# A two-layer encoder on one core: the last quarter of a norm's shift and scale read after the norm, and three up groups interleaved token-major

## The chip, the core and the metric

The kernel runs on one NeuronCore of a Trainium2 chip. A core has TensorE (PE, matrix products, with its weight loads shown apart as PEld), VectorE (DVE), ScalarE (ACT), GpSimd (POOL) and SyncE (SP), which here issues nearly all DMA transfers. Each engine runs its own instructions in a fixed order and waits for others by semaphores. The metric is the device time of one execution in microseconds (us); the number for a kernel is the median of its runs.

## The reference

The model has two layers over 256 tokens of width D = 2048, all in float32. A conditioning vector c sets, for each layer, six vectors of length 2048: shift, scale and gate for the mixer (m) and for the feed-forward part (f).

```python
c_act = jax.nn.silu(c)
for l in range(DEPTH):
    mod = (c_act @ w_mod[l] + b_mod[l]).reshape(bn, 6, d)
    shift_m, scale_m, gate_m = mod[:, 0, None], mod[:, 1, None], mod[:, 2, None]
    shift_f, scale_f, gate_f = mod[:, 3, None], mod[:, 4, None], mod[:, 5, None]
    h = layer_norm(x) * (1.0 + scale_m) + shift_m
    proj = h @ w_in[l]
    ...
    y = jnp.concatenate([y_a, y_b, y_c, y_d], axis=-1) @ w_out[l]
    x = layer_norm(ALPHA * x + (1.0 + gate_m) * y, post_mix_g[l], post_mix_b[l])
    h = layer_norm(x) * (1.0 + scale_f) + shift_f
    y = conv_ffn(h, w_up[l], w_conv[l], b_conv[l], w_down[l])
    x = layer_norm(ALPHA * x + (1.0 + gate_f) * y, post_ffn_g[l], post_ffn_b[l])
```

`conv_ffn` multiplies h by w_up (2048 by 11264), splits the result into a gate and a value half of 5632 columns, runs a causal convolution of width 3 and a SiLU over the gate half, multiplies the two halves and multiplies by w_down. w_mod has 2048 rows and 12288 columns a layer, 100 MB in float32; w_up has 92 MB a layer.

## The kernel before

**Products.** A weight block of 128 rows is one step of the inner dimension, numbered kt from 0 to 15 for an inner dimension of 2048. A product is done in one of two ways. *Exact*: both operands in float32; the trace shows two records for each product of 512 columns, and the weights (`wexact`) come by DMA straight into the tile that PE reads. *Split*: both operands are split into a high and a low part, and three products are added: high by high, high by low, low by high. ACT casts the raw weights `wraw` to the high part `whi`, DVE subtracts to get the low part `wlo`, in pieces of 128x1024; `weights` does both. Activations have the same pair (`hT` from the normed rows `hN`, `a` from the mixers' outputs or the gated values).

**Orientation.** `group2` makes a group of 512 up columns feature-major: the weights are the stationary operand, and the result has features on partitions, which is what the convolution over tokens needs. `first_group` makes the first group of a layer token-major: the normed rows are stationary, the weights stream, and two results (128 tokens each) are turned by four PE transposes each (`ps_gT`) into the gate tile.

**Modulation.** w_mod is too large to be read at once. `mod_stream` is a generator: a step transfers one block of 128 rows by 2048 columns (1 MB) and DVE multiplies it by one entry of c_act per partition and adds it to `macc` (128x2048). After 16 steps PE sums the partitions by one-column products with ones (`ps_mod`, line 79 in `sum_cols`, two records for each of 16 columns). `pump` calls the stream at a rate for each stage, given in RATES: so many steps for each unit of weights. `need` runs the stream until a vector that is wanted is there.

**Buffers and queues.** Raw weights, mod blocks and the norms' gain and bias rows share one ring of four buffers of 1 MB. SP issues their transfers in program order, and each waits until DVE has let go of the buffer. The order of instructions on an engine is set by the program and the framework's scheduler, before the run.

**Layer 0 around the change.** The out-projection has 2048 output columns in chunks: 0 to 1023 split (four sums `o_000`, `o_001`, `o_010`, `o_011`: token half and column quarter), 1024 to 1535 exact and 1536 to 2047 exact (`plain`). After each chunk `finish` does, for each sum, a product with the gate (`yg`), the residual (`x`) and the statistics (`st`) on DVE. Then the norm of the mixer and the norm before the feed-forward part follow, the second with shift_f and scale_f. The normed rows are transposed by PE (`ps_xT`), ACT and DVE apply scale and shift (`hN`), DVE makes the low parts (`hT`), and PE runs the first up group exactly. Then the up groups follow in turn: gate group (`g_c`), value group (`v_c`), eleven of each, and the down projection `d`, chunked as the out-projection is.

## Time and profile before

| | |
|---|---|
| median of 3 runs | 2292.62 us (2290.36 to 2293.0) |
| profiled execution | 2285.5 us |
| its span, first to last instruction | 2283.7 us |
| mean granted TensorE clock | 0.991 |
| PE busy | 2226.7 us (98%) |
| DVE busy | 1788.8 us (78%) |
| ACT busy | 1049.8 us (46%) |
| mean DMA rate | 265 GB/s |

Times in the profile count from the start of the span. A row of the timeline has the start, the busy time, the engine, the line, the operation with its tiles and shapes, how many instructions are merged into it, and in brackets the idle time just before it and who ended that. A row of a group has a count, the busy time with the mean of one in ns, and the idle time before. The out-projection of layer 0 starts at 325.36, the norm's transposes at 440.87, the down projection's first chunk ends near 1078.

### The profile page before, as it was taken

Reading aid. Unit: us, or ns where it says so; the run is one execution under the profiler, and the core shown is the slowest. Engines: PE = TensorE matmul, PEld = TensorE weight load, DVE = VectorE, ACT = ScalarE, POOL = GpSimd, SP = SyncE. Lnnn points to the kernel's source line nnn. Section 1 sums busy time; section 2 is a strip of 40 time slices with the busy share of each in tenths; the row PEclk is TensorE's granted clock in tenths of the full one; section 3 lists DMA queues with packets and bytes.
Section 4 is the critical chain, followed back from the end, with each engine's and each line's share of the span. In section 5 each row is a group of like instructions: output and inputs, shape, how many; then the busy total and the mean of one; then the engine's idle time right before and its main releaser. Section 6 shows DMA issues by size and latency. Waiting matters only on the chain. (4 is left out here: it accounts for less than half of the span.)

```text
span 2283.7 us, 30024 instructions
## 1 busy us (share of the span) xinstructions
PE 2226.7 (98%) x11682; PEld 1859.8 (81%) x11682; DVE 1788.8 (78%) x2270; ACT 1049.8 (46%) x1525; POOL 35.3 (2%) x59
## 2 busy tenths in 40 slices
PE   5899999999999999999999999999999999999998
PEld 4688886478888888887887999877888888888886
DVE  6878998598888898998976799787776565665676
ACT  2221141355554544544556434556555554454553
POOL 2000000000000000000000000000000000000000
PEclk9999999999999999999999999999999999999999
DMA  9999889778998988888974666876765556555554
GB/s 348 368 335 342 304 301 393 301 267 304 319 329 302 323 312 327 317 316 304 319 258 148 200 214 240 291 268 223 247 223 190 184 182 199 186 196 190 193 194 147
DMA packets 224566, 605.21 MB, mean 265 GB/s; under 512 B 14548, under 2 KB 27076, under 8 KB 202660
## 3 DMA queue, kind: packets, MB, share of 16 engines
q1 hardware_dynamic: 223576, 602.30, 74.7%
q8 instruction: 91, 1.49, 0.3%
q0 software_dynamic: 848, 1.01, 0.1%
q14 instruction: 51, 0.42, 0.0%
HBM read 601.16 MB, written 2.10 MB: 264 GB/s over the span
## 5 line engine op out<-in xcount | busy, mean ns | idle before, releaser
L456 DVE TENSOR_TENSOR wlo<-wraw,whi 128x1024 fp32r<-128x1024 f32 (+1 forms) x624 | 749.6, 1214 | 315.5 <-ACT whi L455 309.4
L455 ACT CAST whi<-wraw 128x1024 fp32r<-128x1024 f32 (+1 forms) x624 | 649.2, 1047 | 727.2 <-PE g_c L79 204.4
L79 PE MATMUL v_c<-hT,whi 128*128 128x512 f32 x1408 | 493.1, 394 | 0.0
L79 PE MATMUL g_c<-hT,whi 128*128 128x512 f32 x1280 | 448.2, 394 | 0.0
L79 PE MATMUL v_c<-hT,wlo 128*128 128x256 f32 x1408 | 394.3, 280 | 0.0
L79 PE MATMUL d<-whi,a 128*128 128x512 f32 x1344 | 387.9, 390 | 0.0
L235 DVE SCALAR_TENSOR_TENSOR macc<-wmod,cact,macc 128x2048 f32<-128x2048 f32 x150 | 351.6, 2344 | 17.1 <-DMA wmod<-in_w_mod_dram 16.8
L79 PE MATMUL g_c<-hT,wlo 128*128 128x256 f32 x1280 | 358.4, 280 | 0.0
L79 PEld LDWEIGHTS v_c<-hT,whi 128*128 128x128 f32 x1408 | 263.9, 187 | 61.0
L79 PEld LDWEIGHTS d<-whi,a 128*128 128x128 f32 x1344 | 252.9, 188 | 52.4
L79 PEld LDWEIGHTS g_c<-hT,whi 128*128 128x128 f32 x1280 | 239.9, 187 | 55.6
L79 PEld LDWEIGHTS v_c<-hT,wlo 128*128 128x128 f32 x1408 | 265.8, 189 | 0.2
L79 PEld LDWEIGHTS g_c<-hT,wlo 128*128 128x128 f32 x1280 | 241.7, 189 | 0.2
L79 PE MATMUL d<-wlo,a 128*128 128x512 f32 x672 | 233.8, 390 | 1.9 <-DVE wlo L456 1.9
L79 PEld LDWEIGHTS d<-wlo,a 128*128 128x128 f32 x672 | 126.6, 188 | 29.1 <-DVE wlo L456 2.7
L79 PE MATMUL o<-whi,a 128*128 128x512 f32 x352 | 102.3, 398 | 2.3 <-ACT whi L455 2.3
L834 DVE SCALAR_TENSOR_TENSOR convD<-gluD,pm,convD 128x237 f32<-128x237 f32 (+26 forms) x240 | 99.0, 458 | 0.5
L474 ACT CAST a<-g 128x512 fp32r<-128x512 f32 x132 | 81.1, 616 | 36.7 <-PE d L79 34.2
L79 PE MATMUL D_c<-hT,whi 128*128 128x256 f32 x448 | 85.7, 292 | 4.0 <-ACT hT L474 3.0
L475 DVE TENSOR_TENSOR a<-g,a 128x512 fp32r<-128x512 f32 x132 | 87.5, 683 | 1.8 <-ACT a L474 1.8
L566 PE MATMUL first<-wexact,hN 128*128 128x512 f32 x192 | 85.7, 596 | 1.5 <-ACT hN L82 1.2
L235 DVE SCALAR_TENSOR_TENSOR qacc<-wmod,cact,qacc 128x1024 f32<-128x1024 f32 (+1 forms) x75 | 80.2, 1070 | 2.4 <-DMA wmod<-in_w_mod_dram 0.4
(311 smaller groups left out, 2462.3 us busy)
## 6 DMA issues: line engine op xcount, KB each, us to landing
wraw<-in_ffn_w_up_dram SPq DMA_DIRECT2D x168, 1024.0 KB, 5.2
wmod<-in_w_mod_dram SPq DMA_DIRECT2D x160, 1024.0 KB, 6.6
wraw<-in_ffn_w_down_dram SPq DMA_DIRECT2D x88, 1024.0 KB, 5.3
wmod<-in_w_mod_dram SPq DMA_DIRECT2D x64, 512.0 KB, 7.9
wraw<-in_w_in_dram SPq DMA_DIRECT2D x30, 1024.0 KB, 5.5
wexact<-in_w_in_dram SPq DMA_DIRECT2D x52, 512.0 KB, 6.7
wraw<-in_w_out_dram SPq DMA_DIRECT2D x24, 1024.0 KB, 7.3
wexact<-in_w_out_dram SPq DMA_DIRECT2D x16, 512.0 KB, 11.0
```

Of the source, the lines that this page charges most:

```text
L79: pe.matmul(o, lhsT, rhs, start=start, stop=stop, skip_group_check=True)
L235: i = dve.scalar_tensor_tensor(out=acc, in0=w, scalar=col, in1=acc, op0=ALU.mult, op1=ALU.add)
L455: held(act.copy(hi[:, :m], r), "cast")
L456: i = dve.tensor_tensor(out=lo[:, :m], in0=r, in1=hi[:, :m].bitcast(F32), op=ALU.subtract)
L474: act.copy(hi, src)
L475: dve.tensor_tensor(out=lo, in0=src, in1=hi.bitcast(F32), op=ALU.subtract)
L566: i = pe.matmul(ps, hN[kt // 4][:, kt % 4, t * P : (t + 1) * P], parts[kt], start=kt == 0, stop=kt == KT - 1, skip_group_check=True,)
L834: dve.scalar_tensor_tensor(out=yd[:, j, 30 - k :], in0=glu[:, j, : S - 30 + k], scalar=CW(k, j), in1=yd[:, j, 30 - k :], op0=ALU.mult, op1 ...
```

## The change

Only layer 0 is rewritten. Of the blocks of shift_f and scale_f the first 12 of 16 (1536 of 2048 columns) are read, summed and applied ahead of the norm, as the whole was. The last quarter is read behind the norm, in eight transfers of 1 MB (four row blocks by 512 columns), alternating between shift and scale, with 32 mod steps 512 wide, and before the steps for gate_f.

The normed rows of the last quarter come later, from `after_norm`. So the first up group (g0) runs exactly over 12 blocks and waits with its sums open. Beside it the value group v0 and the gate group g1 are made token-major by the new `token_group`, each of four units of four blocks: v0 units 0, 1, 2, then g1 units 0, 1, then the rest of the norm is placed, g1 unit 2, then the last units of g0, v0 and g1. All three are turned by transposes. The remaining groups are as before.

The third quarter of w_out (columns 1024 to 1535) is split instead of exact. The rates are 1.1 for the new stage "first", 0.76 instead of 0.7 for the up stage and 0.72 instead of 0.7 for the down stage.

```diff
-    dict(B=1.3, C=1.6, out=2.1, up=0.7, down=0.7),
+    dict(B=1.3, C=1.6, out=2.1, first=1.1, up=0.76, down=0.72),
...
+LATE_KT = 12
...
-            chores.append(lambda: sum_cols(l, m, 0, acc))
+            chores.append(lambda: sum_cols(l, m, k0, acc[:, k0 * P : k1 * P]))
...
         for l, m in order:
-            while chores or len(late) == 2:
+            if (l, m) == (0, GATE_F):
+
+                for u in range(4):
+                    for v, acc in held_back.items():
+                        raw = raw_tile("wmod").rearrange("p (k c) -> p k c", k=4)
+                        nc.sync.dma_start(
+                            out=raw,
+                            in_=A["w_mod"][0, 4 * u * P : 4 * (u + 1) * P, v * D + LATE_KT * P : (v + 1) * D].rearrange(
+                                "(k p) c -> p k c", p=P
+                            ),
+                        )
+                        for k in range(4):
+                            mod_step(acc[:, LATE_KT * P :], raw[:, k, :], 4 * u + k, u + k == 0)
+                        if u == 3:
+                            late.append((0, v, acc, LATE_KT, KT))
+                        yield
...
+            k1 = KT
+            if l == 0 and m in (SHIFT_F, SCALE_F):
+                held_back[m], k1 = acc, LATE_KT
+            w = k1 * P
...
-                nc.sync.dma_start(out=raw, in_=A["w_mod"][l, kt * P : (kt + 1) * P, m * D : (m + 1) * D])
+                nc.sync.dma_start(out=raw[:, :w], in_=A["w_mod"][l, kt * P : (kt + 1) * P, m * D : m * D + w])
...
-                mod_step(acc, raw, kt, kt == 0)
+                mod_step(acc[:, :w], raw[:, :w], kt, kt == 0)
...
+    def token_group(w, c0, name, sums, then):
+
+
+        def products(item, u):
+            if not sums:
+                sums.extend(acc_tile(f"{name}{t}") for t in range(2))
+            for k, (hi, lo) in enumerate(item):
+                kt = 4 * u + k
+                xh, xl = (h[:, kt % 2, :] for h in hT[kt // 2][:2])
+                for t in range(2):
+                    tok = slice(t * P, (t + 1) * P)
+                    mm(sums[t], xh[:, tok], hi, kt == 0, False)
+                    mm(sums[t], xh[:, tok], lo, False, False)
+                    mm(sums[t], xl[:, tok], hi, False, kt == KT - 1)
...
+        def unit(u):
+            stream(lambda: weights(w, 4 * u, 4, c0, 512), lambda item: products(item, u))
...
+        def valued_tokens(t, ps):
+            if t == 0:
+                drain_background()
+            g = G[0][:, :, t * P : (t + 1) * P]
+            dve.tensor_tensor(out=g, in0=g, in1=turned(ps), op=ALU.mult)
...
+            sums = first_group(w, 0, None, LATE_KT // 4)
+            g0, end_g0 = token_group(w, 0, "g0", sums, lambda t, ps: gated_tokens(0, t, ps))
+            v0, end_v0 = token_group(w, D_FF, "v0", [], valued_tokens)
+            g1, end_g1 = token_group(w, 512, "g1", [], lambda t, ps: gated_tokens(1, t, ps))
+            for unit, u in ((v0, 0), (v0, 1), (v0, 2), (g1, 0), (g1, 1)):
+                unit(u)
+            pending.append(after_norm.pop())
+            g1(2)
+            phase(l, "up")
+            g0(3)
+            pending.append(end_g0)
+            v0(3)
+            g1(3)
+            pending.extend([end_v0, end_g1])
+            done = 2
...
+        def rest(rs):
+            needs(l, m_shift, m_scale)()
+            for q in range(quarters, 4):
+                for t in range(2):
+                    to_hN(t, q, rs[t], l, m_shift, m_scale)
+            split_pairs(4 * quarters, KT)
...
-            needs(l, SHIFT_F, SCALE_F),
-            modulated(l, SHIFT_F, SCALE_F),
-            plain=(1024, 1536) if l == 0 else (),
+            needs(l, SHIFT_F, SCALE_F, k1=LATE_KT if l == 0 else KT),
+            modulated(l, SHIFT_F, SCALE_F, LATE_KT // 4 if l == 0 else 4),
+            plain=(1536,) if l == 0 else (),
```

Below are three places as the two programs have them, in rows of an engine's own order: line, operation, result and operands, shape, and a count where a row stands for several instructions.

VectorE at the end of the first half of the out-projection, before: `wlo` is the low part of a piece of w_out, `macc` a mod step, and `yg`, `x`, `st` the finish of the sums `o_000` to `o_011`.

```order
L456 TENSOR_TENSOR wlo<-wraw,whi 128x1024 x2
L235 SCALAR_TENSOR_TENSOR macc<-wmod,cact,macc 128x2048
L660 TENSOR_TENSOR yg<-o_000_2073,gate_2_1866 128x512
L660 TENSOR_TENSOR yg<-o_001_2074,gate_2_1866 128x512
L235 SCALAR_TENSOR_TENSOR macc<-wmod,cact,macc 128x2048
L661 SCALAR_TENSOR_TENSOR x_88<-x_88,yg 128x512
L235 SCALAR_TENSOR_TENSOR macc<-wmod,cact,macc 128x2048
```

No low part follows here, since the third quarter has none. The same place in the changed kernel:

```order
L479 TENSOR_TENSOR wlo<-wraw,whi 128x1024 x2
L237 SCALAR_TENSOR_TENSOR macc<-wmod,cact,macc 128x1536
L712 TENSOR_TENSOR yg<-o_000_2073,gate_2_1866 128x512
L237 SCALAR_TENSOR_TENSOR macc<-wmod,cact,macc 128x1536
L713 SCALAR_TENSOR_TENSOR x_88<-x_88,yg 128x512
L237 SCALAR_TENSOR_TENSOR macc<-wmod,cact,macc 128x1536
L716 BN_STATS st_o_2039<-x_88 128x6
L712 TENSOR_TENSOR yg<-o_001_2074,gate_2_1866 128x512
L712 TENSOR_TENSOR yg<-o_010_2075,gate_2_1866 128x512
L479 TENSOR_TENSOR wlo<-wraw,whi 128x1024 x2
```

Two mod steps and five operations of the finish now stand between the first complete sum and the low parts of the third quarter.

VectorE behind the norm, before: `hT` is the split of the normed rows, the `macc` steps are those of gate_f, and `wlo` belongs to the first value group.

```order
L475 TENSOR_TENSOR hT<-hN_2659,hT 128x2x256
L233 TENSOR_SCALAR macc<-wmod,cact 128x2048
L475 TENSOR_TENSOR hT<-hN_2659,hT 128x2x256
L235 SCALAR_TENSOR_TENSOR macc<-wmod,cact,macc 128x2048
L456 TENSOR_TENSOR wlo<-wraw,whi 128x1024
L235 SCALAR_TENSOR_TENSOR macc<-wmod,cact,macc 128x2048
L456 TENSOR_TENSOR wlo<-wraw,whi 128x1024
```

The changed kernel there, up to the last step of shift's late quarter, whose sums follow:

```order
L498 TENSOR_TENSOR hT<-hN_2734,hT 128x2x256
L235 TENSOR_SCALAR macc<-wmod,cact 128x512 x2
L498 TENSOR_TENSOR hT<-hN_2734,hT 128x2x256
L237 SCALAR_TENSOR_TENSOR macc<-wmod,cact,macc 128x512 x7
L479 TENSOR_TENSOR wlo<-wraw,whi 128x1024
L237 SCALAR_TENSOR_TENSOR macc<-wmod,cact,macc 128x512
L479 TENSOR_TENSOR wlo<-wraw,whi 128x1024
L237 SCALAR_TENSOR_TENSOR macc<-wmod,cact,macc 128x512 x6
L479 TENSOR_TENSOR wlo<-wraw,whi 128x1024 x2
L237 SCALAR_TENSOR_TENSOR macc<-wmod,cact,macc 128x512 x4
L479 TENSOR_TENSOR wlo<-wraw,whi 128x1024 x2
L237 SCALAR_TENSOR_TENSOR macc<-wmod,cact,macc 128x512 x8
```

The six low parts are v0's; the steps in between are those of the late quarter of shift and scale.

VectorE at the end of the first chunk of layer 0's down projection, before:

```order
L456 TENSOR_TENSOR wlo<-wraw,whi 128x1024 x2
L660 TENSOR_TENSOR yg<-d_000_7244,gate_5_4009 128x512
L660 TENSOR_TENSOR yg<-d_001_7245,gate_5_4009 128x512
L661 SCALAR_TENSOR_TENSOR x_88<-x_88,yg 128x512 x2
L664 BN_STATS st_d_7213<-x_88 128x6 x2
L660 TENSOR_TENSOR yg<-d_010_7246,gate_5_4009 128x512
L660 TENSOR_TENSOR yg<-d_011_7247,gate_5_4009 128x512
L661 SCALAR_TENSOR_TENSOR x_89<-x_89,yg 128x512 x2
L664 BN_STATS st_d_7214<-x_89 128x6 x2
L235 SCALAR_TENSOR_TENSOR macc<-wmod,cact,macc 128x2048
L456 TENSOR_TENSOR wlo<-wraw,whi 128x1024 x4
```

In the changed kernel the different rate puts the steps elsewhere:

```order
L712 TENSOR_TENSOR yg<-d_000_7348,gate_5_4414 128x512
L712 TENSOR_TENSOR yg<-d_001_7349,gate_5_4414 128x512
L479 TENSOR_TENSOR wlo<-wraw,whi 128x1024 x2
L713 SCALAR_TENSOR_TENSOR x_88<-x_88,yg 128x512 x2
L716 BN_STATS st_d_7317<-x_88 128x6 x2
L712 TENSOR_TENSOR yg<-d_010_7350,gate_5_4414 128x512
L712 TENSOR_TENSOR yg<-d_011_7351,gate_5_4414 128x512
L713 SCALAR_TENSOR_TENSOR x_89<-x_89,yg 128x512 x2
L716 BN_STATS st_d_7318<-x_89 128x6 x2
L479 TENSOR_TENSOR wlo<-wraw,whi 128x1024 x2
L237 SCALAR_TENSOR_TENSOR macc<-wmod,cact,macc 128x2048
```

Two low parts moved ahead of most of the finish, and the mod step moved behind the next two.

More of the change, by code (lines that the diff above doesn't have):

```diff
@@ L553, in encoder_kernel, with first_group @@
     hN, first = [], []
-    def first_group(w, c0, then):
-        parts = []
-        for u in range(KT // 4):
+    def first_group(w, c0, then, units=KT // 4):
+        parts, sums = [], []
+        for u in range(units):
             parts.extend(p for p, _ in weights(w, 4 * u, 4, c0, 512, True, int(u < 3)))
@@ L563, in products @@
             ps = acc_tile(f"first{t}")
+            sums.append(ps)
             made = []
-            for kt in range(KT):
+            for kt in range(4 * units):
                 i = pe.matmul(
@@ L575, in first_group, with end @@
         flush()
[L576 removed]
+        for u in range(units):
             pump()
+        return sums
+    def token_group(w, c0, name, sums, then):
[10 more added lines that the diff above has]
+                    mm(sums[t], xl[:, tok], hi, False, kt == KT - 1)
+        def end():
+            for t in range(2):
+                then(t, sums[t])
+        def unit(u):
+            stream(lambda: weights(w, 4 * u, 4, c0, 512), lambda item: products(item, u))
+        return unit, end
     def run(g):
@@ L1418, in then @@
                 new_hT()
-                for kt in range(0, KT, 2):
-                    split(hT[kt // 2], hN[kt // 4][:, kt % 4 : kt % 4 + 2, :])
+                split_pairs(0, 4 * quarters)
+                if quarters < 4:
+                    after_norm.append(lambda: rest(rs))
         return then
```

89 lines of the change are left out of this document (52 added, 37 removed).

## The prediction

> **What bounds the kernel now.** First the busy shares of the page, then the stretches around the norm, the waits of TensorE there, and the timelines of the places that the change rewrites.
>
> ```profile
> PE 2226.7 (98%) x11682; PEld 1859.8 (81%) x11682; DVE 1788.8 (78%) x2270; ACT 1049.8 (46%) x1525; POOL 35.3 (2%) x59
> ...
> 325.36:380.60 55.24, 52.13 (x227) 41.35 (x225) 49.75 (x45) 18.63 (x25) 0.00 (x0) 0.94 0.91 340
> 380.60:440.87 60.27, 60.27 (x160) 28.47 (x161) 40.37 (x52) 6.69 (x18) 1.49 (x2) 0.97 0.97 380
> 440.87:474.49 33.62, 32.49 (x102) 15.66 (x101) 23.31 (x43) 24.35 (x52) 1.53 (x2) 1.00 0.34 116
> 474.49:520.67 46.18, 46.18 (x268) 40.18 (x266) 43.10 (x51) 23.56 (x34) 0.00 (x0) 1.00 0.92 331
> 520.67:1010.00 489.33, 489.33 (x2721) 423.40 (x2720) 437.70 (x470) 252.21 (x357) 0.00 (x0) 1.00 0.89 317
> ```
>
> PE is the bound (98%), so the time moves only by PE work removed or by waits of PE. The columns after the length are busy PE, PEld, DVE, ACT, POOL, then the granted clock, DMA share and GB/s. The rows are the first half of layer 0's out-projection (columns 0 to 1023), its second half, the norm with the first up group, the next two up groups, and the rest of the up stage. In the last two DVE is busy 93% and 89%, nearly the second bound. In the third it is not, since it waits for the norm. Call the end of the second row, 440.87, T: there the norm's first transposes start.
>
> ```profile
> 353.82 3.15 PE L79 MATMUL ps_mod<-ones,macc 128*128 128x1 f32 x27
> 356.83 1.88 PE L79 MATMUL o<-whi,a 128*128 128x512 f32 x4
> ...
> 365.29 0.73 PE L79 MATMUL o<-wlo,a 128*128 128x512 f32 x2 [0.63 <-DVE wlo L456]
> ...
> 366.78 0.62 PE L79 MATMUL o<-wlo,a 128*128 128x512 f32 x2
> ...
> 368.15 0.62 PE L79 MATMUL o<-wlo,a 128*128 128x512 f32 x2
> ...
> 372.85 1.19 PE L79 MATMUL o<-whi,a 128*128 128x512 f32 x4 [2.27 <-ACT whi L455]
> ...
> 377.62 0.62 PE L79 MATMUL o<-whi,a 128*128 128x512 f32 x2
> ...
> 428.87 5.29 PE L79 MATMUL o<-wexact,yb 128*128 128x512 f32 x8
> 434.00 3.60 PE L79 MATMUL o<-wexact,yc 128*128 128x512 f32 x8
> 437.44 3.60 PE L79 MATMUL o<-wexact,yd 128*128 128x512 f32 x8
> ```
>
> Between 366.78 and 368.15 stand six split products: 0.228 us each. An exact record takes (437.44 − 434.00)/8 = 0.43, a product has two. After 2.27 us of waiting at 372.85, twelve split products took 4.77 us up to 377.62 instead of 2.74: 2.0 lost to a lower clock. After the shift's column sums (32 records, about 3.6 us with their first five) the same shows at 356.83, and after the scale's at 428.87 (eight records 5.1 instead of 3.4: 1.7 lost). The first half therefore holds 192 × 0.228 = 43.7 of products and 3.6 of sums; of its 55.2, 7.9 is waiting or slow clock.
>
> **The change, up to the norm.** (1) The third quarter (columns 1024 to 1535) goes from 64 exact records to 96 split products: 27.5 to 21.9, −5.6. (2) The sums for shift and scale have 12 columns each, not 16: 16 records fewer before T, 16 × 0.1125 = −1.8. (3) Thirty-two steps of the mod stream lose a quarter of their elements and of their megabyte, 8.4 MB in all; at the 380 GB/s of the second half that is 22 us of DMA time, most of it ahead of T.
>
> ```profile
> L235 DVE SCALAR_TENSOR_TENSOR macc<-wmod,cact,macc 128x2048 f32<-128x2048 f32 x28 | 65.7, 2345 | 1.1 <-DMA wmod<-in_w_mod_dram 1.0
> L456 DVE TENSOR_TENSOR wlo<-wraw,whi 128x1024 fp32r<-128x1024 f32 x31 | 36.8, 1217 | 4.3 <-ACT whi L455 4.3
> L235 DVE SCALAR_TENSOR_TENSOR qacc<-wmod,cact,qacc x75: 741/1277/1286, 15.2 to 147.1; 128x1024 f32<-128x1024 f32 x45, 128x512 f32<-128x512 f32 x30
> ```
>
> A 2048-wide step takes 2.35, a 1024-wide 1.28, a 512-wide 0.74 (the last row gives least, median and most of two widths), so a 1536-wide lies between, 1.8: DVE is freed of 32 × 0.55 = 17.6, and gets back eight low parts at 1.2 for the third quarter, 9.7, in the second half where 20 of its 60 us are idle (ACT's eight casts there stand beside 7 busy of 60). Both waits of the first half (the late raw weights behind the 2.27, the late low part behind the 0.63) go with their slow clock: of the 7.9 I take 7.0 off, since the slow spell after 24 records of sums is between that after 32 (1.7) and none; half, 0.85, is kept. The same at the scale's sums, −0.85.
>
> (4) A wait is added at the boundary into the third quarter. It now needs low parts, and on DVE the finish of the first half and three mod steps stand ahead of them. The nearest row is the same boundary in the down projection:
>
> ```profile
> 1069.29 1.29 DVE L660 TENSOR_TENSOR yg<-d,gate 128x512 f32<-128x512 f32 x2 [0.18 <-PE d L79]
> ...
> 1076.47 2.33 DVE L235 SCALAR_TENSOR_TENSOR macc<-wmod,cact,macc 128x2048 f32<-128x2048 f32 x1
> 1078.73 4.62 DVE L456 TENSOR_TENSOR wlo<-wraw,whi 128x1024 fp32r<-128x1024 f32 x4
> 1080.00 0.50 PE L79 MATMUL d<-wlo,a 128*128 128x512 f32 x1 [1.91 <-DVE wlo L456]
> ...
> 1083.87 0.49 PE L79 MATMUL d<-whi,a 128*128 128x512 f32 x1
> ```
>
> There twelve finish operations and a mod step cost PE 1.91, and up to 1083.87 half rate. At the new boundary DVE starts when the first sum is complete, ten products (2.3) before PE is through; five finish operations at 0.64 (two in 1.29), two mod steps behind it at 1.8 and the low part at 1.2 end 5.7 after PE; PE has two products and one exact (1.3) to go on with. The wait is 4.4, with 2.0 of slow clock as at 372.85. Behind it the other units wait less: 0.6 and 0.6, as at 365.29. Ends: 1.9 (the down boundary) and 8 (the whole block). Queued behind on DVE is the rest of the finish, which nobody waits for before T.
>
> Sum to T: −5.6 − 1.8 − 7.0 − 0.85 + 4.4 + 2.0 + 1.2 = −7.7; ends −12 and −4.
>
> **The change, behind the norm.** Today the next two groups end at 520.67, T + 79.8. Work: the last four blocks of the first group go from 16 exact records to 24 split products, −1.4; two groups turned token-major, 2 × 96 × 0.228 = 43.8 against
>
> ```profile
> 477.24 0.39 PE L79 MATMUL v_c<-hT,whi 128*128 128x512 f32 x1
> ...
> 482.09 0.39 PE L79 MATMUL v_c<-hT,whi 128*128 128x512 f32 x1
> ```
>
> fourteen pairs in 4.85, 64 pairs in 22.2 a group, −0.6; 16 more transposes at 0.11, +1.8; the 16 records of sums that come back, +1.8. Together +1.6, and less waiting in the shorter norm, −0.7.
>
> The waits come from DVE, which must now do the late quarter there: eight transfers of 1 MB, 32 steps, and behind them low parts for v0.
>
> ```profile
> 458.27 1.04 PE L612 MATMUL ps_xT<-cst,xn 128*128 128x128 f32 x8
> ...
> 468.10 0.68 DVE L475 TENSOR_TENSOR hT<-hN,hT 128x512 fp32r<-128x512 f32 x1
> ```
>
> The split of the normed rows ends at 468.78, T + 27.9. With 12 blocks the first half of the exact group is 8 records (3.4) and a set of transposes (0.4) shorter, and four operations of 0.4 to 0.7 and a 1.28 step go: T + 20.6. From there to the last step of the shift DVE has two first steps (0.5), 26 steps at 0.75 and six low parts at 1.17: 27.5, so T + 48.1. PE, by its own work, has 24 transposes, 48 exact records and 1.5 of waits, T + 24.7, then three units of v0 at 24 × 0.228: T + 41.1. So PE loses 7.0 before the shift's sums, most of it at low parts of v0, then some 0.9 at g1's first, and 0.9 of slow clock (between none and 4). Stretch: +1.6 − 0.7 + 7.0 + 0.9 + 0.9 = +9.7; ends +1 (no wait) and +13 (slow clock in full). The gate's steps that used to run here come later, in the up stage: at a pace of 0.76 instead of 0.7 its DVE share goes from 0.89 to about 0.92 and stays covered by PE's products (489 of 489 busy); +0.5 for the first group, ends 0 and 1.5.
>
> **The down boundary.** The order puts two low parts ahead of the finish there and the mod step behind: the 1.91 and its slow clock go, −3.5 (ends −4 and 0). Nothing else of layer 1 moves.
>
> Sum: −7.7 + 9.7 + 0.5 − 3.5 = −1.0 on the profiled 2285.5 (span 2283.7). The median is 7 above that run; I put −1.0 on it: 2291.6. A measurement here tells 0.2% (4.6 us) from no change.
>
> [...] At 1080.00 the clock fell after 1.91 us of idle. [...]
>
> **The rivals.** *DVE gets through (faster).* If the 512-wide steps of the two accumulators overlap, they could cost what a 2048-wide row pays per 512 columns beyond its fixed part, (2.35 − 0.74)/3 = 0.54: 26 × 0.21 = 5.5 less, with the 0.9 + 0.9 behind it: −7.3, 2284.3. It decides when the shift's last step ends before T + 41. For it: the finish operations run at 0.64 back to back. Against: steps of one accumulator depend on each other, and the 0.74 is from such a row.
>
> *The clock holds (faster).* The stalls stay, but none lowers the clock. That takes away 2.0 + 0.9 + 0.85 + 0.85 = 4.6: 2287.0. Against: 372.85 and 1080.00.
>
> *Late transfers (slower).*
>
> ```profile
> wraw<-in_ffn_w_up_dram SPq DMA_DIRECT2D x168, 1024.0 KB, 5.2
> ...
> wexact<-in_w_out_dram SPq DMA_DIRECT2D x16, 512.0 KB, 11.0
> ```
>
> ```profile
> SPq L346 <- DVE x L701: 21.1, 1, 21.1
> ```
>
> The eight late transfers and v0's raw weights share four raw buffers, and each is issued by SP only when DVE has let go of one. If one lands as late as the exact w_out pieces, 11.0 instead of 5.2, DVE itself stands: 5.8 and 2.0 of slow clock, +7.8, 2299.4. It decides once a transfer comes later than the 3.0 of its predecessor's four steps. For it: SP stood 21.1 us behind the norm's DVE work for one mod transfer, so DMA's share was 0.34 there. Against: the same 0.34 leaves the DMA engines free, and all buffers come free with the norm. POOL has only the two root steps of the norm and is passed by nothing.
>
> *The norm doesn't come earlier (slower).* If the boundary block costs its full 8 and the low parts of the third quarter keep waiting, T moves by −2: +4.7, 2296.3 or somewhat more.
>
> **Chances.** The sum as it stands 0.46 (its own range 2285 to 2298; 0.04 of it faster, 0.04 slower), DVE through 0.24, clock 0.10, late transfers 0.14, no earlier norm 0.06. Faster 0.04 + 0.24 + 0.10 = 0.38; slower 0.04 + 0.14 + 0.04 = 0.22; within 0.2% 0.40. The range leaves a tenth of the chance beyond each end: 2281.5 to 2300.
>
> **What would show it.** Right: T near 433; a wait of 3 to 5 of PE for a low part at the boundary after the first half, none for a cast within it; DVE without a gap from the end of the norm to the shift's sums, and PE waiting there for low parts and for the accumulator; no wait at the down boundary. Wrong: PE waits under 2 us in all behind the norm, or DVE there waits for transfers, or T later than 437.

## The result

The changed kernel is slower: 2297.47 us (median of 20 runs, 2291.08 to 2304.07) against 2287.95 us (20 runs, 2282.67 to 2293.0); the ratio is 1.004, 95% interval 1.003 to 1.005. The forecast was 2291.6 and "no change"; it stood on a median of 2292.62 from three runs of the kernel before, which twenty runs put at 2287.95.

The profiled execution of the changed kernel took 2291.08 us (span 2289.3), the least of its 20 runs. Both kernels were therefore profiled a second time, among the runs below: 2304.71 us (span 2302.9) and 2287.1 us (span 2285.3). The stages follow from where each one's first product starts; the rows are those of the stretches (length, busy PE, PEld, DVE, ACT, POOL, granted clock as a share of the full one, DMA share, GB/s). The changed kernel, first profile: the output projection, the norm with the first three up groups, the rest of the up stage.

```profile
PE 2224.5 (97%) x11674; PEld 1869.2 (82%) x11674; DVE 1801.3 (79%) x2306; ACT 1054.2 (46%) x1531; POOL 35.4 (2%) x59
...
326.77:435.10 108.33, 104.18 (x403) 74.30 (x402) 84.48 (x101) 32.97 (x49) 1.49 (x2) 0.95 0.86 310
435.10:521.10 86.00, 79.98 (x322) 56.15 (x321) 71.94 (x105) 45.19 (x77) 1.54 (x2) 0.98 0.75 271
521.10:957.40 436.30, 433.75 (x2477) 378.59 (x2476) 393.91 (x432) 221.72 (x328) 0.00 (x0) 1.00 0.89 320
```

The changed kernel, second profile, with the projection stage ahead of the output projection (called C below, after its groups) as the first row:

```profile
236.80:334.30 97.50, 94.71 (x434) 78.54 (x434) 83.02 (x143) 23.70 (x45) 3.69 (x2) 0.96 0.79 280
334.30:441.00 106.70, 102.89 (x402) 73.06 (x401) 84.43 (x101) 32.53 (x47) 1.49 (x2) 0.97 0.88 315
441.00:527.00 86.00, 79.97 (x323) 56.19 (x322) 72.00 (x106) 45.22 (x77) 1.54 (x2) 0.98 0.75 271
527.00:964.80 437.80, 435.17 (x2477) 379.81 (x2476) 393.87 (x432) 221.90 (x327) 0.00 (x0) 0.99 0.89 319
```

The kernel before, second profile, the same four stretches:

```profile
236.10:329.80 93.70, 92.86 (x435) 77.31 (x434) 84.81 (x141) 22.22 (x42) 3.69 (x2) 0.98 0.84 307
329.80:447.80 118.00, 113.92 (x387) 70.60 (x386) 89.94 (x96) 26.12 (x44) 1.49 (x2) 0.94 0.92 353
447.80:527.36 79.56, 78.05 (x366) 55.75 (x364) 66.29 (x93) 46.93 (x84) 1.54 (x2) 1.00 0.67 240
527.36:953.10 425.74, 425.74 (x2459) 375.07 (x2458) 380.99 (x417) 224.29 (x323) 0.00 (x0) 1.00 0.89 321
```

The output projection is shorter by 9.2 (mean of two and two: 107.5 against 116.8). Everything around it is longer: stage C by 2.4 (94.9 against 92.5), the three groups behind the norm by 6.3 (86.0 against 79.7), the rest of the up stage by 8.8 (437.1 against 428.2), and the second layer, from its stage C on, by 2.9 (948.8 against 945.9). Only the stretch from the start of the down projection to there is as long as before (386.2 against 386.3). With 0.5 ahead of stage C the means of the two pairs differ by 11.6 us, the medians by 9.5. In the first profiles TensorE is busy as long as before (2224.5 against 2226.7) and waits more; in the second it is also busy longer (2231.7 against 2225.0).

The waits of TensorE in the changed kernel, first profile, from the start of the output projection to the end of the third group and on to the down projection:

```profile
375.64 1.02 PE L81 MATMUL o<-wexact,ya 128*128 128x512 f32 x2
380.24 0.50 PE L81 MATMUL o<-wlo,a 128*128 128x512 f32 x1 [3.58 <-DVE wlo L479]
...
462.14 0.50 PE L81 MATMUL v<-wlo,hT 128*128 128x512 f32 x1 [1.69 <-DVE wlo L479]
...
468.69 0.73 PE L81 MATMUL v<-whi,hT 128*128 128x512 f32 x2 [1.24 <-ACT whi L478]
...
483.35 1.05 PE L81 MATMUL ps_mod<-ones,macc 128*128 128x1 f32 x8 [1.05 <-DVE macc L237]
...
485.80 0.50 PE L81 MATMUL g<-wlo,hT 128*128 128x512 f32 x1 [0.82 <-DVE wlo L479]
...
763.25 1.38 PE L81 MATMUL ps_mod<-macc,cst 128*128 128x16 f32 x8 [2.44 <-DVE macc L216]
764.47 2.05 PE L81 MATMUL v_c<-hT,whi 128*128 128x512 f32 x4
...
1086.01 0.50 PE L81 MATMUL d<-wlo,a 128*128 128x512 f32 x1 [1.92 <-DVE wlo L479]
```

The 3.58 is the new boundary wait. Of the four behind the norm two are for low parts, one (1.05) is for the last step of the shift's late quarter, and one (1.24) is for a cast, whose raw weights came late:

```profile
460.32 0.37 SPq L464 DMA_DIRECT2D wraw<-in_ffn_w_up_dram  x1
467.59 2.00 ACT L478 CAST whi<-wraw 128x1024 fp32r<-128x1024 f32 x2 [11.18 <-DMA wraw<-in_ffn_w_up_dram]
```

SP issued this transfer when a narrow mod step had let go of a buffer (460.30), and it landed at 467.51. The 2.44 at 763.25 was in no term of the forecast: there TensorE waits for the folded sums of a vector of layer 1 (`fold_cols`, line 216), in the rest of the up stage, where the kernel before has no wait at all. On VectorE a mod step stands ahead of the last operation of the fold:

```profile
758.21 1.24 DVE L215 STREAM_TRANSPOSE turned<-macc 128x1024 f32<-128x1024 f32 x1
...
759.73 2.34 DVE L237 SCALAR_TENSOR_TENSOR macc<-wmod,cact,macc 128x2048 f32<-128x2048 f32 x1
761.99 1.21 DVE L216 TENSOR_REDUCE macc<-turned 128x32 f32<-128x1024 f32 x1
```

The 1.92 is the down projection's boundary, which was to lose its wait.

VectorE behind the norm shows the chain that the forecast laid out:

```profile
456.23 4.72 DVE L237 SCALAR_TENSOR_TENSOR macc<-wmod,cact,macc 128x512 f32<-128x512 f32 x7
460.87 1.22 DVE L479 TENSOR_TENSOR wlo<-wraw,whi 128x1024 fp32r<-128x1024 f32 x1
...
477.17 6.13 DVE L237 SCALAR_TENSOR_TENSOR macc<-wmod,cact,macc 128x512 f32<-128x512 f32 x8
```

Seven narrow steps (0.67 each) stand ahead of v0's first low part. The last eight (0.77) end at 483.3, 48.2 after the norm's transposes.

The largest piece of what parts the two profiles of the changed kernel, 5.3 of 13.6 us, stands in stage C. The second profile, TensorE and then VectorE:

```profile
323.63 0.61 PE L81 MATMUL ps_var<-ones,sqD 128*128 128x1 f32 x4 [2.53 <-ACT sqD L911]
...
326.85 3.76 PE L81 MATMUL C_c<-hF,wexact 128*128 128x256 f32 x8
```

```profile
320.43 1.82 DVE L237 SCALAR_TENSOR_TENSOR macc<-wmod,cact,macc 128x1536 f32<-128x1536 f32 x1 [3.37 <-DMA wmod<-in_w_mod_dram]
322.17 1.41 DVE L906 SCALAR_TENSOR_TENSOR convD<-ps_mean,convD 128x256 f32<-128x256 f32 x4
```

and the kernel before, first profile, at the same place:

```profile
318.58 0.50 PE L79 MATMUL ps_var<-ones,sqD 128*128 128x1 f32 x4
...
323.82 1.89 PE L79 MATMUL C_c<-hF,wexact 128*128 128x256 f32 x8
```

VectorE stands for 3.37 us in front of a 1536-wide mod step whose transfer has not landed. The conformer branch's mean subtraction (`convD`) is queued behind that step, ACT squares its result, and PE waits for the squares; eight records then take 3.76 us, twice the 1.89 of eight in the kernel before: the granted clock was 0.5 from 325.70 to 332.53. The longer wait (1.7) and this clock (3.4) make nearly all of the 5.3 us: in the first profile the same wait was 0.8, no such clock stood behind it, and the stage took 92.2.

### The profile page after: what moved, and what is told of

It is laid out like the page before. It is cut to its first block, busy times and chain, and to the rows that moved or that the text cites. A ratio compares the mean times of both kernels' runs of the same rounds, so it can differ in the third digit from the quotient of the medians.

```text
span 2289.3 us, 30028 instructions
## 1 busy us (share of the span) xinstructions
PE 2224.5 (97%) x11674; PEld 1869.2 (82%) x11674; DVE 1801.3 (79%) x2306; ACT 1054.2 (46%) x1531; POOL 35.4 (2%) x59
## 3 DMA queue, kind: packets, MB, share of 16 engines
q0 software_dynamic: 848, 1.01, 0.1%
## 5 line engine op out<-in xcount | busy, mean ns | idle before, releaser
L81 PE MATMUL v_c<-hT,whi 128*128 128x512 f32 x1344 | 468.6, 395 | 0.0
L81 PE MATMUL g_c<-hT,whi 128*128 128x512 f32 x1216 | 423.1, 393 | 0.0
L81 PE MATMUL v_c<-hT,wlo 128*128 128x256 f32 x1344 | 371.8, 281 | 0.1
L237 DVE SCALAR_TENSOR_TENSOR macc<-wmod,cact,macc 128x2048 f32<-128x2048 f32 (+2 forms) x180 | 357.5, 1990 | 14.6 <-DMA wmod<-in_w_mod_dram 13.7
L81 PE MATMUL g_c<-hT,wlo 128*128 128x256 f32 x1216 | 337.4, 280 | 0.0
L81 PEld LDWEIGHTS v_c<-hT,whi 128*128 128x128 f32 x1344 | 251.6, 188 | 55.7
L81 PEld LDWEIGHTS g_c<-hT,whi 128*128 128x128 f32 x1216 | 227.3, 187 | 51.1
L81 PEld LDWEIGHTS g_c<-hT,wlo 128*128 128x128 f32 x1216 | 229.2, 189 | 1.0
L497 ACT CAST a<-g 128x512 fp32r<-128x512 f32 x132 | 81.2, 618 | 93.7 <-PE d L81 89.4
L81 PE MATMUL o<-whi,a 128*128 128x512 f32 x416 | 122.3, 397 | 0.1
L81 PEld LDWEIGHTS o<-whi,a 128*128 128x128 f32 x416 | 79.4, 191 | 17.9 <-ACT whi L478 1.0
```

The costliest lines, as they stand in the source:

```text
L81: pe.matmul(o, lhsT, rhs, start=start, stop=stop, skip_group_check=True)
L237: i = dve.scalar_tensor_tensor(out=acc, in0=w, scalar=col, in1=acc, op0=ALU.mult, op1=ALU.add)
L497: act.copy(hi, src)
```

## The experiments

The ratios are to the kernel before on the same chip, with 95% intervals; the changed kernel is at 1.004 (1.003 to 1.005).

### The third quarter exact again, and the split alone

```diff
-            plain=(1536,) if l == 0 else (),
+            plain=(1024, 1536) if l == 0 else (),
```

> The changed kernel with the third quarter of the first output projection exact again (late quarter and token-major groups stay). Theory: the split saves 5.6 us of products, but its wait for low parts at the boundary (3.6 us in the changed kernel) and the lowered clock behind it (about 2) give that back, so this version runs within 2 us of the changed kernel, about 9 us over the kernel before, and has no wait at that boundary. Rival: the split is a gain of its own, and taking it back costs 5.6 us: about 15 us over the kernel before.

Measured: 2298.28 us, 1.0048 (1.0031 to 1.0066), as the theory had it. The output projection had no wait of TensorE and took 107.4, as long as with the split. The 5.6 us of the split pay for its boundary wait and no more.

The reverse, the kernel before with the split and nothing else:

```diff
-            plain=(1024, 1536) if l == 0 else (),
+            plain=(1536,) if l == 0 else (),
```

> The kernel before with the third quarter split and nothing else. Theory: 5.6 us of products go, a wait of about 4 us for low parts at the boundary comes with about 2 us of lowered clock: within 2 us of the kernel before. Rival: the boundary is hidden: 5 to 6 us faster. If so, the late quarter alone is the cause of the loss.

Measured: 2289.9 us, 1.0008 (0.9995 to 1.0022): the theory's time, but not its wait. Without the relief of the narrow steps the boundary's wait is for casts, and through them for weights that land late:

```profile
382.84 1.22 PE L79 MATMUL o<-whi,a 128*128 128x512 f32 x2 [4.38 <-ACT whi L455]
```

### A quarter of the late steps

```diff
-                        for k in range(4):
+                        for k in range(1):
                             mod_step(acc[:, LATE_KT * P :], raw[:, k, :], 4 * u + k, u + k == 0)
```

> The changed kernel in which only one of the four mod steps of each late transfer is done, 8 of 32 (the late quarter of shift and scale is wrong, all transfers stay). Theory: VectorE's late steps are what PE waits for behind the norm; with 18 us less of them the 5.3 us of waits there and their lowered clock (about 2) go: 6 to 8 us less than the changed kernel, 2 to 3 over the kernel before. Rival: the transfers or the casts are late as well, the waits stay by more than half: at most 3 us less than the changed kernel.

This kernel leaves out three of every four late steps, so its shift and scale are incomplete.

Measured: 2291.35 us, 1.0021 (1.0009 to 1.0033), 4 us less than the changed kernel by the ratios and 6 by the medians, between theory and rival by the ratios. The three groups behind the norm took 81.0 instead of 86.0, and of the waits there little is left, with all transfers still made:

```profile
PE g L81 <- ACT whi L478: 0.8, 1, 0.8
PE g L81 <- DVE wlo L479: 0.5, 1, 0.5
PE ps_xT L664 <- ACT xn L84: 0.5, 1, 0.5
```

So VectorE's 32 steps are what TensorE waits for there, by their own time and by the buffers that they hold; this run doesn't part the two. The number of transfers alone is not the cause. Stage C took 97.0 here too, so the other loss is apart from this one.

### The paces back

```diff
-    dict(B=1.3, C=1.6, out=2.1, first=1.1, up=0.76, down=0.72),
+    dict(B=1.3, C=1.6, out=2.1, first=1.1, up=0.7, down=0.7),
```

> The changed kernel with the up and down rates at 0.7 as before. Theory: the wait of 2.4 us for the folded sums in the up stage and the lowered clock behind it come from where the new pace puts the fold; they go, about 3 us less than the changed kernel, about 6 over the kernel before, while the wait at the down projection's first boundary stays between 2 and 4 us. Rival: the fold waits somewhere else instead, since VectorE is nearly full either way: within 1.5 us of the changed kernel.

Measured: 2297.07 us, 1.0044 (1.003 to 1.0058): the rival. The wait for the fold in the up stage was gone (the rest of the up stage took 430.2 instead of 436.3), and another stood ahead of the next layer, where the norm waits for the steps that the slower pace had not done:

```profile
PE ps_xT L664 <- ACT xn L84: 3.6, 2, 3.1
```

The wait at the down projection's boundary was 1.4, less than the theory's 2 to 4.

### The shift read whole; a slower stream in stage C

Only the scale's last quarter is held back:

```diff
-            if l == 0 and m in (SHIFT_F, SCALE_F):
+            if l == 0 and m == SCALE_F:
                 held_back[m], k1 = acc, LATE_KT
...
-                need(l, m, k1)
+                need(l, m, KT if m == SHIFT_F else k1)
```

> The changed kernel in which only the scale's last quarter comes behind the norm; the shift is read whole ahead of it, so the steps of the projection stage before the output projection are 2048 wide as in the kernel before, and VectorE has their order of before there. Theory: in the profiles of three versions with the late quarter the output projection began 6 to 7 us later than before (332.5 instead of 325.4), since VectorE there stands in front of a narrow mod step whose transfer has not landed while the conformer branch's mean subtraction is queued behind it; with wide steps it begins at 325 to 327 again, and with 16 late steps instead of 32 the waits behind the norm fall from 5.3 us to under 2: 8 to 11 us less than the changed kernel, within 3 us of the kernel before. Rival: the later beginning is spread over runs and has nothing to do with the narrow steps: it stays at about 332, and only 3 to 5 us are won.

Measured: 2312.79 us, 1.0123 (1.01 to 1.0145). Of the theory only the first half held: with VectorE's order of before, stage C took 91.3. But the output projection took 115.8, as long as before, the groups behind the norm 86.9 in spite of half the late steps, and a fold in the down projection made TensorE wait as long as nowhere else:

```profile
PE ps_mod L81 <- DVE macc L216: 5.0, 1, 5.0
```

The pace of stage C at 1.3 instead of 1.6:

```diff
-    dict(B=1.3, C=1.6, out=2.1, first=1.1, up=0.76, down=0.72),
+    dict(B=1.3, C=1.3, out=2.1, first=1.1, up=0.76, down=0.72),
```

> The changed kernel with the pace of the mod stream in that projection stage at 1.3 instead of 1.6, so that fewer narrow steps stand ahead of the mean subtraction. Theory (mod steps and their transfers delay the conformer branch): the output projection begins 3 to 6 us earlier than in the other versions with the late quarter, and the steps that are left over fit into the output projection, where VectorE has room: 3 to 6 us less than the changed kernel. Rival: within 1.5 us of it, the wait stays or moves to the output projection.

Measured: 2301.81 us, 1.0073 (1.0055 to 1.0092), worse than the changed kernel. Stage C took 92.2 with a wait of 0.4 for the squares, as the theory said. But VectorE had no room in the output projection: TensorE waited there 5.5 us for a mod step, ahead of column sums. Steps that were put off also came back in the up stage: 443.2 instead of 436.3 there, with waits for low parts. First the one, then the other:

```profile
PE ps_mod L81 <- DVE macc L237: 5.5, 1, 5.5
...
PE v_c L81 <- DVE wlo L479: 2.9, 2, 2.5
```

### Low parts first at the two boundaries

The finish of the first chunk of both projections is ordered behind the low parts of the next chunk's first unit, its second half behind those of the second unit.

```diff
+                g = dve.tensor_tensor(out=y, in0=p, in1=box["gate"][:, cols], op=ALU.mult)
+                if c0 == 0 and name in ("o0", "d0"):
+                    tc.add_manual_dep(g.ins, last_split[0], order_dep, reason="the next products wait for their low parts")
...
+                    if t == 1 and c0 == 0 and name in ("o0", "d0"):
+                        deferred.append(lambda: finish(1, state["ps"], c0))
+                        continue
```

> The changed kernel with one order changed: the finish of the first chunk of both projections of layer 0 stands behind the low parts of the next chunk's first unit, its second half behind those of the second unit. Theory: the waits of 3.6 us at the output projection's boundary and 1.9 us at the down projection's go, with up to 2 us of lowered clock each: 5 to 9 us less than the changed kernel. Rival: VectorE is nearly full, the finish is needed soon after, and the waits come back at another unit: under 3 us are won.

Measured: 2292.95 us, 1.0029 (1.0016 to 1.0043). The waits at both boundaries were gone; the whole output projection kept these:

```profile
PE o L81 <- DVE wlo L483: 0.8, 2, 0.5
PE o L81 <- ACT whi L482: 0.3, 1, 0.3
```

and it took 103.8. By the ratios 2.5 us are won (by the medians 4.5), less than the theory's 5; the intervals overlap. The same with the kernel before, first with the split, then at the down boundary alone:

> The kernel before with the third quarter split and the same order at both boundaries; no late quarter, no token-major groups. Theory: the 5.6 us of the split are won without the boundary's wait, and the down boundary's 1.9 us with its lowered clock too: 6 to 10 us faster than the kernel before. Rival: the mod stream at full width leaves VectorE and the transfers no room in the output projection, so that the wait for casts (6.3 us in the version with the split alone) stays: at most 3 us faster.

Measured: 2290.69 us, 1.0016 (1.0003 to 1.0029), the rival: the wait at the boundary stayed 4.67 us, for a cast, since the weights land late there.

> The kernel before with one order changed, at the first boundary of layer 0's down projection: the finish of the first chunk behind the low parts of the next chunk's units, in two halves. Theory: the wait of 1.9 us and its lowered clock go and nothing else moves: 2 to 4 us faster than the kernel before. Rival: the wait comes back at a later unit, since VectorE has to do the same work in the same time: within 1.5 us of it.

Measured: 2286.64 us, 1.0001 (0.9988 to 1.0015), the rival. The 1.9 us were gone from the profile and 0.8 stood in its place, but the time did not move: at most 2.7 us can have been there to win.

### The second profiles

> The changed kernel itself, for a second profile, since the first profiled execution (2291.1 us) was the fastest of its 20. Theory: what it lacks against the median stands ahead of the output projection: that begins at 330 to 333 us instead of 326.8, behind a wait of 2 to 3 us for the conformer branch's squares and a lowered clock, and the rest of the stages is within 2 us of the first profile. Rival: the lacking 6 us are spread over all stages (lowered clock after any wait): the output projection begins before 329 and no stage differs by more than 3.

Measured: 2304.71 us. The output projection began at 334.3, later than the theory's 330 to 333, behind the wait of 2.53 us shown above; the output projection and the groups behind it were within 2 us of the first profile, and layer 1 from its stage C on took 950.6 instead of 947.0, so that the theory holds for the largest piece only.

> The kernel before itself, for a second profile, to see how far a stage differs from run to run without the change. Theory: the output projection begins at 325 to 327, the norm's transposes stand 115 to 118 behind it, and the up stage has no wait of TensorE. Rival: the stages before the output projection spread by 5 us here as well, and the later beginning in the changed versions says nothing.

Measured: 2287.1 us. The output projection began at 329.8, between theory and rival: stage C took 93.7 here, and no wait for the squares was in it; the granted clock was 0.5 from 238.45 to 241.86. The norm's transposes stood 118.0 behind, and the up stage had no wait of more than 0.7.

### Both orders and the pace, and the mean subtraction first

The low parts first and the paces back together:

> The changed kernel with the low parts first at both boundaries and the up and down paces back at 0.7. Theory: the two gains add, 4.5 us by the boundaries and 5 us by the fold's wait in the up stage (2.4 of waiting and as much of lowered clock at 760 us in the changed kernel, absent in the profile at the old pace): 2286 to 2290 us, within 2 us of the kernel before. Rival: at the old pace the steps that the up stage doesn't take are missing at the end of layer 0, where the next norm waits for them, and nothing is won over the version with the low parts first: about 2293.

Measured: 2289.97 us, 1.0019 (1.0007 to 1.0031): 3.4 us over the kernel before, at the slow end of the theory's 2286 to 2290 but not within its 2 us of the kernel before, and the best of the versions with the late quarter. C took 92.7, the output projection 103.4, the groups behind the norm 86.6, and ahead of the second layer the norm's wait of 3.1 was there.

Stage C's order alone: its chores are placed ahead of the mod steps of the same unit, and the next four steps are ordered behind the subtraction.

```diff
+        if mods and not chores_first[0]:
+            pump()
         for _ in range(min(bg, len(background))):
             background.pop(0)()
+        if mods and chores_first[0]:
+            pump()
...
+            if l == 0:
+                hold["mod"] = [sub.ins.name, 4]
```

> The changed kernel with one order changed in the projection stage ahead of layer 0's output projection: the conformer branch's mean subtraction on VectorE stands ahead of the narrow mod steps instead of behind three of them. Theory: the wait of 2.5 us for the squares and the lowered clock behind it (the stage took 97.5, 98.2, 97.0 and 95.0 us in four profiles of versions with the late quarter, 91.3 to 93.7 in the versions without) go: the stage takes 91 to 93 us, and the time is 3 to 6 us less than the changed kernel's. Rival: the stage's length varies for other reasons, or the steps that move back are missing in the output projection: within 1.5 us of the changed kernel.

Measured: 2302.26 us, 1.0072 (1.0048 to 1.0095), worse. Stage C took 93.2 without any wait for the squares, so the order is the cause of that wait. It is not the order of before either: 24 mod steps stand ahead of the subtraction, 27 in the kernel before and 29 in the changed kernel. The output projection took 120.1 in the profiled execution (2316.04 us, the slowest of the six), with TensorE waiting for casts, which wait for w_out transfers. That these land late because the steps now hold their raw buffers longer, ahead of them on SP's queue, is argued and not shown:

```profile
PE o L81 <- ACT whi L482: 8.6, 4, 4.4
...
ACT whi L482 <- DMA wraw<-in_w_out_dram: 46.5, 7, 10.9
```

> The changed kernel with the mean subtraction first, the low parts first at both boundaries and the paces back at 0.7. Theory: the three losses are separate places, so their gains add: the version with the latter two is 3.4 us over the kernel before, less 3 to 5: between 2 us faster and 1 slower than the kernel before; what remains is the waits for VectorE behind the norm. Rival: they hide one another: no less than 3 us over the kernel before.

Measured: 2295.09 us, 1.0034 (1.0022 to 1.0046), the rival. C 92.8, output projection 115.4, again with 8.3 us of waits for casts.

> The same with an up pace of 0.73 and a down pace of 0.72. Theory: the fold's place depends on the pace step by step, so that between 0.7 (wait of 3.1 us at the second layer's norm) and 0.76 (2.4 us in the up stage) neither need wait: 1 to 4 us less than with 0.7, and faster than the kernel before. Rival: VectorE is full, and one of the two waits is there at any pace: within 1.5 us of the version with 0.7.

Measured: 2297.8 us, 1.0042 (1.0026 to 1.0057), the rival. Instead of one of the two waits there was a third, of 3.1 us for a low part of a value group:

```profile
PE v_c L81 <- DVE wlo L487: 3.1, 1, 3.1
```

No version ran measurably faster than the kernel before.

## Why the prediction was wrong

The forecast's sum was −1.0; measured are 9.5 us. The steps that failed are the up stage, +0.5 by the forecast and 8.8 between the means of the profiles, and the down boundary, −3.5 by the forecast and nothing in the profiles. By the forecast's own steps:

**Up to the norm: right where it looked, and one stage short.** The output projection alone changed by −9.2 (107.5 against 116.8), the forecast had −7.7. Its wait at the boundary was 3.58 and 2.9 us against 4.4; behind the first, fourteen split products took 4.88 us instead of 3.2, 1.7 of lowered clock against 2.0. But the step "thirty-two steps of the mod stream lose a quarter" was carried out only for the output projection. Sixteen of these steps are the shift's, and most of them stand in stage C, which the forecast didn't cost at all. The order there did change. VectorE's listing before, with the number of the row first:

```
292 L834 SCALAR_TENSOR_TENSOR convD<-gluD,pm_102,convD 128x226
293 L235 SCALAR_TENSOR_TENSOR macc<-wmod,cact,macc 128x2048
...
295 L235 SCALAR_TENSOR_TENSOR macc<-wmod,cact,macc 128x2048
296 L854 SCALAR_TENSOR_TENSOR convD<-ps_mean,convD 128x256 x4
```

and after:

```
293 L886 SCALAR_TENSOR_TENSOR convD<-gluD,pm_102,convD 128x226
294 L237 SCALAR_TENSOR_TENSOR macc<-wmod,cact,macc 128x1536 x2
...
296 L237 SCALAR_TENSOR_TENSOR macc<-wmod,cact,macc 128x1536
297 L906 SCALAR_TENSOR_TENSOR convD<-ps_mean,convD 128x256 x4
```

A third mod step came to stand between the last `gluD` row and the subtraction (29 ahead of it in all, not 27), and its transfer is the one that is late. In the seven profiles with that order the stage took 92.2, 97.5, 98.2, 93.5, 97.0, 95.0 and 92.7, with waits of 0.5 to 2.7 for the squares; in the three with the subtraction first 93.2, 92.8 and 91.4, with none. That the wait comes from this order is shown. The stage's length also moves without it: the kernel before took 91.3 and 93.7. And in the runs that put the subtraction first the output projection lost more than stage C gained (115.4 to 120.1 against 107.5). Over both stages the changed kernel gains 6.8 (202.4 against 209.2), the forecast's 7.7 nearly, but as 9.2 won and 2.4 lost.

**Behind the norm: right in the mechanism.** The last step of the shift was to end 48.1 after the transposes; it ended 48.2 after. That this agrees to 0.1 is luck: the split of the normed rows ended at T + 21.2 instead of 20.6, and seven of the narrow steps took 0.67 and not 0.75. The stretch was to be 9.7 longer; it is 6.3, and 2.2 to 2.6 us more of its work (16 transposes and most of the parameter rows) stood behind its end: the first group of the up stage took 24.76 us, a plain one 22.19 to 22.61. TensorE was to lose 7.0 before the shift's sums; they began at 483.35, T + 48.3, so it lost 7.2 against its own T + 41.1. But the waits in that are only 4.5. The lowered clock, 1.7 for the half rate from 470.30 to 473.71, lies within the loss, where the forecast had added 0.9 of it on top. The run with a quarter of the steps shows that the narrow steps cause the loss.

**The up stage: wrong.** The term was +0.5, argued from VectorE's share of 0.92 "covered by PE's products". Measured are 5.5 between the first profiles and 12.1 between the second, of which 2.2 to 2.6 is the work just named. A share is a mean, and what counts is where one piece falls: at the new pace a fold of four operations on VectorE, with a mod step among them, comes when TensorE has already reached its sums: 2.44 us of waiting at 763 and 1.7 of lowered clock (3.41 us at 0.5), in the second profile 2.44 and 3.4 (6.83 us at 0.5). The rest goes with the pace of products that wait for nothing (last section); the kernel before alone took 430.7 and 425.7. At the old pace that place is free, and the second layer's norm waits 3.1 instead. The forecast named the pace and looked at no fold. That the fold's wait costs the kernel its time is not shown, since the run without it was no faster.

**The down boundary: wrong in the step, and the prize was not there.** The term was −3.5. The low parts ahead of the finish were only those of the first unit; the second unit's stood behind the other ten operations, and TensorE waited 1.92 for these, at 1086.01. In the kernel before, with the wait taken away for both units, the time was the same (1.0001).

**The second layer: 2.9 longer,** without a wait to show for it, and in no term of the forecast. Most of it is the pace of the last section: in the second profile of the changed kernel the first eight groups of the second layer's up stage ran at the slower of two paces (472.9 us for the stage, against 469.6 in the first and 469.2 twice in the kernel before).

**The rivals.** None came about as priced. DVE did not get through, and the clock did not hold (0.5 for 3.41 us from 381.55 and from 470.30). Late transfers stood behind the norm in a smaller way than the rival had it: VectorE waited only 0.31 and 0.75 us for casts of late weights, TensorE 1.24. The slower side came by places that no rival named: the fold in the up stage, the down boundary that gave nothing back and, for a smaller part, the third mod step in stage C. Of the signs given, "T near 433" held roughly in the first profile (435.1) and failed in the second (441.0), where the forecast's own sign, "later than 437", marked it wrong.

**The clock.** Slow clock behind waits did come, as in the kernel before behind the 1.91 us of idle at 1080.00, but not behind each. In the first profile of the changed kernel 3.58 us of idle at 380.24 and 2.44 at 763.25 were followed by half rate (0.5 for 3.41 us from 381.55 and from 763.84), and 1.69 at 462.14 and 1.92 at 1086.01 were not (1.00 up to 465.60 and to 1089.40).

## What to carry to other kernels

When a change makes a streamed step smaller, follow every stage in which such steps stand, not only the one it is meant for: a scheduler may put one more of them ahead of work that others wait for. Where the engine that feeds TensorE is busy nine tenths of the time, as VectorE was here (393.91 of 436.30 us in the up stage), a wait that is taken away at one place may return at the next (at the old pace the 2.44 us at the fold were gone and 3.1 stood ahead of the next norm), and a price for a wait read from one profile may be more than its removal brings: the 1.9 us here brought nothing measurable. A static order has to be read through to the second unit behind a boundary.

## What was unexpected of the hardware

The pace of products that wait for nothing varied by about 1% between executions at a granted clock of 1.00: in the kernel before the stretch from the first value group to the down projection took 476.9 and 472.3 us in two profiles, without a wait above 0.7 us in either. A feature-major group of 64 pairs took 22.19 or 22.61 us, for several groups on end. Ten groups of layer 0 took 22.61 or 22.62 in the first profile of the kernel before, none in the second. The same gate group (`g_c`) in both, over its whole length:

```profile
543.27:565.88 22.61, 22.61 (x130) 19.60 (x129) 18.57 (x19) 9.70 (x13) 0.00 (x0) 1.00 0.91 329
549.55:571.73 22.18, 22.18 (x130) 19.56 (x129) 18.53 (x19) 9.71 (x13) 0.00 (x0) 1.00 0.95 336
```

In a stage of 470 us that is as much as a term of the forecast. What sets the pace no run tells.

A low clock behind a wait did not follow from the wait's length alone. The down boundary's wait, 1.91 or 1.92 us in all four profiles of the two kernels, was followed by half rate in the first of the kernel before (0.5 from 1080.67 to 1084.08) and in the second of the changed kernel, and not in the first of the changed kernel. The rows around it, the second profile of the changed kernel and then the first:

```profile
1090.29:1093.70 3.41, 1.49 (x7) 0.95 (x6) 3.41 (x6) 2.56 (x4) 0.00 (x0) 1.00 0.05 22
1093.70:1097.11 3.41, 3.41 (x9) 2.63 (x9) 3.41 (x3) 0.00 (x0) 0.00 (x0) 0.50 0.43 101
...
1081.28:1084.70 3.42, 2.81 (x13) 2.00 (x11) 3.42 (x6) 1.65 (x3) 0.00 (x0) 1.00 0.51 216
1084.70:1088.11 3.41, 2.10 (x9) 1.77 (x10) 3.41 (x4) 1.48 (x2) 0.00 (x0) 1.00 0.00 0
1088.11:1091.52 3.41, 3.41 (x17) 2.83 (x16) 3.41 (x3) 0.82 (x2) 0.00 (x0) 1.00 0.95 334
```

Between 230 and 1340 us the first profile of the kernel before has four spells at 0.5, from 357.05, 374.11, 428.73 and 1080.67, and that of the changed kernel five, from 367.90, 381.55, 422.51, 470.30 and 763.84, each 3.41 us long. Five of the nine came behind or close behind waits: 2.27 and 1.91 us in the kernel before, 3.58, 1.24 with 0.52, and 2.44 in the changed one. The other four came behind 24 or 32 small products for column sums (`ps_mod`) without a wait. So a wait of the same length cost nothing in one profile and 1.7 us of lowered clock in two. What decides it no run tells.
